# Both ends of attention in a two-layer hybrid kernel: loads of the first head, inputs and weights of the output projection, order of its rows

## The chip, the cores and the metric

The kernel runs on one core of one Trainium2 chip. The metric is the device time of one execution in microseconds (us). One core has five engines with an instruction queue each: TensorE (PE, with its weight loads shown apart as PEld), VectorE (DVE), ScalarE (ACT), GpSimd (POOL) and SyncE (SP, which here only issues DMAs). Each queue runs its instructions in the order in which they stand; a semaphore wait in front of one holds all that stand behind it on that engine.

## What is computed

Two layers work on 256 context tokens and 1024 latent tokens of width 1024, in f32. Cut to what matters here:

```python
def layer(x, ctx):
    h = x * (1 + scale) + shift                    # the same for ctx, with its own vector
    ru, rg, aq, ak, av, ag, nq, nk, nv, ng = split(h @ w_in)
    yr = rwkv_bidirectional(ru)                    # 6 heads x 64: 384 columns
    ya = grouped_query_attention(aq, ak, av)       # 6 query and 2 key heads x 64: 384 columns
    yn = neighbourhood_attention(nq, nk, nv, rpb)  # 4 heads x 64: 256 columns
    y = concat(yr * silu(rg), ya * silu(ag), yn * silu(ng)) @ w_out
    return layer_norm(alpha * x + gate * y)
```

The first layer also updates the context tokens; the second gives the latent tokens alone.

## The kernel before, in words

Each layer goes through four stages: the input projections (`layer_proj`), the RWKV branch in waves of chained small steps (`rwkv`), the attention heads (`attention`), and the output projection with the norm (`out_weights`, `out_proj`). The stages are written one after the other, but the order on each engine is decided when the kernel is built: a scheduler simulates the program and places each instruction where it becomes ready, so the last waves run beside the first attention heads, and the first products of the output projection run inside the last attention heads. Pools of tiles reuse each other's addresses with waits by tile, so a tile of a later stage waits for the last reader of what lay there.

**First head of attention.** Heads come in the order 0, 1, 2, 3 (neighbourhood), then the two groups of query heads, G before H in layer 0 and H before G in layer 1. A head's keys and queries lie in DRAM as 64 rows; `dup` (L851) loads them twice into the two halves of a staging tile `stg` (L857, two DMAs), from ACT's queue for the first two calls of a layer and from SP's after that. `load_k` (L860) casts the tile to the reduced format fp32r (ACT, L865) and takes the remainder (POOL, L866); `load_q` (L869) does the same (L873, L874, L875). `na_head` (L1081) calls `load_k`, then `load_q`, then loads values and the two bias tables.

**Between the two.** Each head's last steps (`inv`, `spread`, `gate`) turn sums of the softmax into factors (L1010, L1012, L1015, L1023), multiply (L1025) and store 64 rows of the result to `yg_d` (L1033). `yg_d` has eight rows of 128 features: rows 0 to 2 come from the RWKV branch (L806), 3 to 5 from the grouped heads, 6 and 7 from the neighbourhood heads.

**Output projection.** `out_weights` (L1131) loads `wout` as eight blocks of 128 output features (m0 to m7), 512 KB each, into a staging pool of four buffers (L1137), casts them on ACT (`wh`, L1140) and takes the remainder `wl` on DVE and POOL in turn (L1141). `out_proj` (L1144) goes over blocks of 256 tokens in the order 2, 3, 4, 1 and, in layer 0 alone, 0. For a block, `fetch` loads the eight rows k of `yg_d` one by one (`yf`, 128 KB, two buffers, L1157), casts them (`yh`, ACT, L1160) and takes the remainder (`yl`, POOL, L1161). Each product of an m and a k is three matmuls: yh by wh, yl by wh, yh by wl (L1186, L1187, L1188). The first half of a block is m0 to m3, the second m4 to m7; L1194 adds the half to the residual `s`, 1 MB, three buffers, loaded at L1281. The norm follows (`norm`, and `norm_last` with L1244 for the last block). What sets the order around the change:

```python
kord = (6, 3, 4, 5, 0, 1, 2, 7)                 # rows k of yg_d, in the order of fetch and of the sums
order = [2, 3, 4, 1] + ([] if last else [0])
```

**RWKV.** The wave step `wave_pre` (L555) has a tile `lp` (L578) in the pool `r2`; the blocks of the branch's output with odd number use the same place as `yb` (L772).

## Time and profile before

| | |
|---|---|
| time, median of 3 runs | 2469.1 us (2462.72 to 2471.28) |
| the profiled execution | 2478.63 us, of it 2476.9 us from the first to the last instruction |
| granted clock of TensorE, mean | 0.937 |
| TensorE matmul busy | 2189.6 us (88%) |
| VectorE busy | 1625.1 us (66%) |
| ScalarE busy | 1003.5 us (41%) |
| GpSimd busy | 1184.1 us (48%) |
| DMA | 298.17 MB, 120 GB/s in the mean |
| attention of layer 0 begins, layer 0's output projection follows it | at about 550 us, 1190 us |
| attention of layer 1 begins, layer 1's output projection follows it | at about 1783 us, 2341 us |

The page gives busy time by engine, a row of tenths by slice of the span, and the chain of work that ended last. Rows of the timeline read: start, duration, engine, line, operation, output and input, count; in brackets the engine's idle time before it and who ended it. A row with ACTq or SPq is the issue of DMAs from that queue. Windows give busy time by engine, the granted clock (PEclk, 1.00 is full) and the share of time in which the DMA engines were busy.

### The profile page before, as it was taken

The page shows a single profiled execution, that of the slowest core. Times are in us where ns is not written, and L with a number is a line of the kernel's source. Part 1 is how long each engine was busy: PE and PEld are TensorE (multiplying, and loading weights), DVE is VectorE, ACT ScalarE, POOL GpSimd, SP SyncE. Part 2 cuts the span into 40 slices and gives each one's busy share as a digit, 9 for nine tenths or more (in the row PEclk, how much of TensorE's full clock was granted, in tenths as well). Part 3 has the DMA queues.
Part 4 walks back from the last instruction along what each step waited for, and adds up shares of the span by engine and source line. Part 5 has one row for each costly group of instructions (what it writes and reads, how often), then busy time and mean ns, then how long its engine had stood idle before and what let it go on. Part 6 is the DMA issues. An engine that isn't in the chain of part 4 may idle for free.

```text
span 2476.9 us, 57781 instructions
## 1 busy us (share of the span) xinstructions
PE 2189.6 (88%) x22616; PEld 1645.0 (66%) x22616; DVE 1625.1 (66%) x3063; ACT 1003.5 (41%) x2186; POOL 1184.1 (48%) x1438
## 2 busy tenths in 40 slices
PE   6989999987888888989899999899868788989697
PEld 3777898765555555545897777787645555556397
DVE  5686423545768777775396785525468688778646
ACT  3333413334445454463233434223345444445522
POOL 4464426335555554462245456434456545545433
PEclk9999999996879999998999999999879999999899
DMA  7344335446555444351332445334555545332522
GB/s 281 112 162 164 111 92 123 120 108 139 126 116 136 114 100 119 102 177 34 101 103 91 146 161 182 107 90 121 141 116 140 102 99 117 84 90 64 161 71 94
DMA packets 448241, 298.17 MB, mean 120 GB/s; under 512 B 249600, under 2 KB 395880, under 8 KB 446944
## 3 DMA queue, kind: packets, MB, share of 16 engines
q1 hardware_dynamic: 439936, 281.71, 41.6%
q0 software_dynamic: 7392, 10.28, 1.5%
q8 instruction: 178, 2.92, 0.5%
q10 hardware_dynamic: 640, 2.49, 0.4%
q14 instruction: 95, 0.78, 0.1%
HBM read 198.37 MB, written 91.79 MB: 117 GB/s over the span
## 4 chain that ended last, share of the span: by engine, by line
PE 44%; DVE 21%; DMA 15%; issue 7%; ACT 6%; POOL 4%; SPq 3%; DVEq 0%; POOLq 0%; ACTq 0%
PE pj L203 5%; PE pj L204 5%; PE pj L205 5%; PE y L948 4%; DMA yf<-yg_d 3%; PE st L963 3%; PE sm L894 3%; DMA ls_d<-G 3%; DVE G L625 2%; PE st L964 2%; DVE mx L896 2%; DVE tmp L653 2%; PE ch L734 2%; PE py L754 1%; DMA lin<-ls_d 1%
## 5 line engine op out<-in xcount | busy, mean ns | idle before, releaser
L204 PE MATMUL pj<-hlo,wh 128*128 128x512 f32 (+1 forms) x1072 | 401.4, 375 | 14.3 <-DVE hlo L480 8.0
L203 PE MATMUL pj<-hhi,wh 128*128 128x512 f32 (+1 forms) x1072 | 403.2, 378 | 9.4 <-ACT qr L348 5.2
L205 PE MATMUL pj<-hhi,wl 128*128 128x512 f32 (+1 forms) x1072 | 400.6, 374 | 0.2 <-POOL wl L169 0.2
L204 PEld LDWEIGHTS pj<-hlo,wh 128*128 128x128 f32 x1072 | 205.0, 191 | 56.2 <-DVE hlo L480 8.3
L203 PEld LDWEIGHTS pj<-hhi,wh 128*128 128x128 f32 x1072 | 204.4, 191 | 54.8 <-issue 6.8
L169 POOL TENSOR_TENSOR wl<-wf,wh 128x512 fp32r<-128x512 f32 x104 | 143.8, 1387 | 202.2 <-ACT wh L168 178.7
L896 DVE TENSOR_REDUCE mx<-sm 128x1 f32<-128x512 f32 (+1 forms) x372 | 198.8, 554 | 50.1 <-PE sm L894 47.6
L205 PEld LDWEIGHTS pj<-hhi,wl 128*128 128x128 f32 x1072 | 204.9, 191 | 38.4 <-issue 3.3
L970 ACT ACTIVATE pt<-st 128x512 f32<-128x512 f32 (+1 forms) x292 | 164.9, 583 | 130.1 <-PE st L964 122.8
L948 PE MATMUL y<-pt,v 128*64 128x256 f32 (+1 forms) x1392 | 211.5, 398 | 2.3 <-ACT pt L973 1.4
L894 PE MATMUL sm<-k,q 128*128 128x256 f32 (+2 forms) x436 | 166.1, 422 | 25.8 <-DVE mx L896 19.5
L963 PE MATMUL st<-q,k 128*128 128x512 f32 (+3 forms) x376 | 165.0, 444 | 21.1 <-DVE rc L1012 5.9
L1186 PE MATMUL pj<-yh,wh 128*128 128x256 f32 x576 | 160.2, 290 | 24.4 <-ACT yh L1160 23.1
L1187 PE MATMUL pj<-yl,wh 128*128 128x256 f32 x576 | 164.0, 288 | 0.8 <-POOL yl L1161 0.8
L1188 PE MATMUL pj<-yh,wl 128*128 128x256 f32 x576 | 162.2, 286 | 0.0
L977 POOL TENSOR_TENSOR acc<-acc,pt 128x512 f32<-128x512 f32 x80 | 106.4, 1330 | 102.7 <-ACT pt L970 101.4
L948 PEld LDWEIGHTS y<-pt,v 128*64 128x64 f32 x1392 | 94.0, 142 | 89.6 <-issue 58.0
L964 PE MATMUL st<-q,k 65*128 65x512 f32 (+3 forms) x376 | 146.7, 393 | 1.9 <-ACT q L908 1.2
L894 PEld LDWEIGHTS sm<-k,q 128*128 128x128 f32 x436 | 80.6, 201 | 89.8 <-DVE mx L896 37.0
L625 DVE TENSOR_TENSOR G<-gt,msk 64x192 f32<-64x192 f32 (+1 forms) x320 | 110.5, 345 | 39.7 <-PE gt L620 28.4
L708 POOL MEMSET X<- 32x192 f32 x320 | 81.2, 254 | 102.0 <-PE py L754 74.6
L1186 PEld LDWEIGHTS pj<-yh,wh 128*128 128x128 f32 x576 | 109.9, 196 | 26.0 <-ACT yh L1160 23.5
(276 smaller groups left out, 5104.5 us busy)
## 6 DMA issues: line engine op xcount, KB each, us to landing
wf<-win SPq DMA_DIRECT2D x104, 256.0 KB
wm<-wmod SPq DMA_DIRECT2D x32, 512.0 KB
yf<-yg_d SPq DMA_DIRECT2D x72, 128.0 KB
wt<-wm SPq DMA_DIRECT2D x8, 1024.0 KB
gate_d<-o SPq DMA_DIRECT2D x32, 256.0 KB
wf<-wout SPq DMA_DIRECT2D x16, 512.0 KB
ldkk<-rw_d SPq DMA_DIRECT2D x40, 192.0 KB
ldkd<-rw_d SPq DMA_DIRECT2D x40, 192.0 KB
```

Of the source, the lines that this page charges most:

```text
L203: nc.tensor.matmul(out=ps[:, :n], lhsT=wh, rhs=hhi[:, k, t0:t0 + n], start=(k == 0), stop=False)
L204: nc.tensor.matmul(out=ps[:, :n], lhsT=wh, rhs=hlo[:, k, t0:t0 + n], start=False, stop=False)
L205: nc.tensor.matmul(out=ps[:, :n], lhsT=wl, rhs=hhi[:, k, t0:t0 + n], start=False, stop=(k == KT - 1))
L894: nc.tensor.matmul(out=sp_[:, :o], lhsT=q[0][:, qc:qc + 128], rhs=k[0][:, c0:c0 + o], start=True, stop=True)
L896: nc.vector.tensor_reduce(out=mx[:, n_:n_ + 1], in_=sp_[:, :o], op=ALU.max, axis=AX.X)
L948: mm = nc.tensor.matmul(out=y[64 * i:64 * i + 64, a0:a1], lhsT=v[:, t, :], rhs=pt[:, p0:p0 + a1 - a0], start=start, stop=stop and at == le ...
L963: nc.tensor.matmul(out=o, lhsT=k[0][:, 128 * t:128 * t + 128], rhs=q[0][:, qa:qb], start=True, stop=False)
L964: mm = nc.tensor.matmul(out=o, lhsT=k[1][0:65, 128 * t:128 * t + 128], rhs=q[1][0:65, qa:qb], start=False, stop=True)
L970: nc.scalar.activation(out=pt[:, :w], in_=sp_[:, :w], func=AF.Exp)
L1186: nc.tensor.matmul(out=p_, lhsT=wh[m][:, k], rhs=yh, start=(x_ == 0), stop=False)
L1187: nc.tensor.matmul(out=p_, lhsT=wh[m][:, k], rhs=yl, start=False, stop=False)
L1188: nc.tensor.matmul(out=p_, lhsT=wl[m][:, k], rhs=yh, start=False, stop=(x_ == KT - 1))
```

## The change

Five edits go together:

1. In each layer's first neighbourhood head, the loads of k and q are both issued before the cast of k; the staging tiles are handed to `load_k` and `load_q`.
2. The tile `lp`, and `yb` in its place, lie in pool `r3` instead of `r2`.
3. In the last layer, the pool of `yf`, `yh`, `yl` is opened ahead of the weights' staging pool, so that it has addresses of its own. The staging pool has two buffers there instead of four, and `yf` eight instead of two.
4. The order of the rows k: layer 0 ends with 4 and 5, layer 1 with 3 and 4, the rows that the last attention heads write.
5. Each block's load of the residual `s` is ordered behind the block's last `yf` load so far.

```diff
-                lp = r2.tile([128, 3, 4, 33], F32, tag="lp", name="lp")
+                lp = r3.tile([128, 3, 4, 33], F32, tag="lp", name="lp")
...
             for i in range(2):
-                eng.dma_start(out=sg_[64 * i:64 * i + 64, c0:], in_=src[:, c0:])
-            return sg_
-
-        def load_k(h):
-            sg_ = dup(k_d[h])
+                ld = eng.dma_start(out=sg_[64 * i:64 * i + 64, c0:], in_=src[:, c0:])
+            return sg_, ld
+
+        def load_k(h, sg_=None):
+            sg_ = sg_ or dup(k_d[h])[0]
...
-        def load_q(h):
-            sg_ = dup(q_d[h], lo)
+        def load_q(h, sg_=None):
+            sg_ = sg_ or dup(q_d[h], lo)[0]
...
-            k, q, v = load_k(2 + h), load_q(6 + h), load_v(vn_d, 64 * h)
+            sk = sq_ = None
+            if not nl[0]:
+                sk, sq_ = dup(k_d[2 + h])[0], dup(q_d[6 + h], lo)[0]
+            k, q, v = load_k(2 + h, sk), load_q(6 + h, sq_), load_v(vn_d, 64 * h)
...
-        w0 = est.enter_context(tc.tile_pool(name=f"of{l}", bufs=4, reuse_waits="tile"))
+        last = l == DEPTH - 1
+        w3 = es.enter_context(tc.tile_pool(name=f"oy{l}", bufs=2, reuse_waits="tile")) if last else None
+        w0 = est.enter_context(tc.tile_pool(name=f"of{l}", bufs=2 if last else 4, reuse_waits="tile"))
...
-                yf = w3.tile([128, n], F32, tag="yf", name="yf", bufs=2)
-                nc.sync.dma_start(out=yf, in_=yg_d[k, :, t0:t0 + n])
+                yf = w3.tile([128, n], F32, tag="yf", name="yf", bufs=8 if last else 2)
+                got[b] = nc.sync.dma_start(out=yf, in_=yg_d[k, :, t0:t0 + n])
...
-        kord = (6, 3, 4, 5, 0, 1, 2, 7)
+        kord = ((6, 7, 3, 0, 1, 2, 4, 5), (6, 7, 5, 0, 1, 2, 3, 4))[l]
...
-            nc.sync.dma_start(out=s, in_=x_src[:, :, 256 * b:256 * b + n])
+            follow(nc.sync.dma_start(out=s, in_=x_src[:, :, 256 * b:256 * b + n]), got[b])
```

No engine gets more or fewer instructions. The order changes within attention and output projection of both layers. In the changed kernel the lines of the output projection stand 7 to 10 lower: L1144 for L1137, L1166 for L1157, L1196 to L1198 for L1186 to L1188, L1291 for L1281. Three places follow.

On ACT, where attention of layer 0 begins, before (X, rsb and yst belong to the last RWKV waves; the bracket names the semaphores that the instruction waits on):

```order
L857 DMA stg<-k_d 64x1280 [waits DMAHW1_49]
L857 DMA stg<-k_d 64x1280 [waits DMAHW4_49]
L716 COPY rsb<-ch 128x192 [waits DVE_49,PE_49,Activation_49]
L865 CAST k_9985<-stg 128x1280 [waits DMAHW4_49,DMAHW6_49,DMAHW1_49,DMAHW0_49]
L857 DMA stg<-q_d 64x1280 [waits DMAHW5_49]
L730 COPY X_2966<-ch 32x3x64 [waits PE_49]
L730 COPY X_2966<-ch 32x3x64 x2
L857 DMA stg<-q_d 64x1280 [waits DMAHW7_49]
L873 CAST q_9991<-stg 128x1280 [waits DMAHW7_49,DMAHW5_49]
```

The same place of the changed kernel:

```order
L857 DMA stg<-k_d 64x1280 [waits DMAHW1_49]
L857 DMA stg<-k_d 64x1280 [waits DMAHW4_49]
L857 DMA stg<-q_d 64x1280 [waits DMAHW6_49,DMAHW0_49,DVE_49]
L716 COPY rsb<-ch 128x192 [waits DVE_49,PE_49,Activation_49]
L857 DMA stg<-q_d 64x1280 [waits DMAHW0_49]
L865 CAST k_9988<-stg 128x1280 [waits DMAHW4_49,DMAHW1_49]
L730 COPY X_2966<-ch 32x3x64 [waits PE_49]
L730 COPY X_2966<-ch 32x3x64 x2
L873 CAST q_9991<-stg 128x1280 [waits DMAHW6_49,DMAHW0_49]
L874 COPY q_9992<-q_9991 64x1280 [waits Activation_49]
```

Both loads of q moved up from behind the cast of k; the first now waits on a DVE semaphore and two DMA semaphores of its own.

On PE, right behind the last attention instruction of layer 0 (`tb`), before. The number behind pj names the block m (13764 is m3, 13877 is m4), that behind yh the row k in the order of fetch (13699 the first, 13705 the second, 13711 the third):

```order
L1023 MATMUL tb_13615<-c_ident_62,rb_13612 128x128 x4
L1186 MATMUL pj_13764<-yh_13699,wh_13654 128x256
L1187 MATMUL pj_13764<-yl_13700,wh_13654 128x256
L1188 MATMUL pj_13764<-yh_13699,wl_13655 128x256
L1186 MATMUL pj_13764<-yh_13705,wh_13654 128x256
L1187 MATMUL pj_13764<-yl_13706,wh_13654 128x256
L1188 MATMUL pj_13764<-yh_13705,wl_13655 128x256
L1186 MATMUL pj_13764<-yh_13711,wh_13654 128x256
L1187 MATMUL pj_13764<-yl_13712,wh_13654 128x256
L1188 MATMUL pj_13764<-yh_13711,wl_13655 128x256
L1186 MATMUL pj_13877<-yh_13699,wh_13660 128x256
```

And of the changed kernel, from twelve matmuls further on, with the fifth, sixth and seventh row (13723, 13729, 13735):

```order
L1196 MATMUL pj_13764<-yh_13723,wh_13654 128x256
L1197 MATMUL pj_13764<-yl_13724,wh_13654 128x256
L1198 MATMUL pj_13764<-yh_13723,wl_13655 128x256
L1196 MATMUL pj_13764<-yh_13729,wh_13654 128x256
L1197 MATMUL pj_13764<-yl_13730,wh_13654 128x256
L1198 MATMUL pj_13764<-yh_13729,wl_13655 128x256
L1196 MATMUL pj_13764<-yh_13735,wh_13654 128x256
L1197 MATMUL pj_13764<-yl_13736,wh_13654 128x256
L1198 MATMUL pj_13764<-yh_13735,wl_13655 128x256
L1196 MATMUL pj_13877<-yh_13699,wh_13660 128x256
```

Behind attention, m3 now takes seven rows before m4 begins, where it took three. Ahead of `tb`, among the instructions of the last heads, the products of m0 to m2 stand with the first three rows before (27 matmuls) and with the first seven in the changed kernel (63 matmuls); the one row left is the last in order.

On SP, at the end of attention of layer 1, before:

```order
L1137 DMA wf<-wout 128x1024 [waits DMAHW4_49]
L806 DMA yg_d<-yo 128x3x128 [waits DMAHW5_49,DVE_49,Activation_49]
L1137 DMA wf<-wout 128x1024 [waits DMAHW6_49,DMAHW1_49,DVE_49]
L1137 DMA wf<-wout 128x1024 [waits DMAHW7_49,DMAHW2_49,Pool_49]
L1137 DMA wf<-wout 128x1024 [waits DMAHW3_49,DMAHW0_49,DVE_49]
L1137 DMA wf<-wout 128x1024 [waits DMAHW4_49,Pool_49]
L1033 DMA yg_d<-gtl 64x512 [waits DVE_49]
L1033 DMA yg_d<-gtl 64x512
L1281 DMA s<-x_d 128x8x256 [waits DMAHW2_49,DMAHW3_49,PE_49,Pool_49]
L1281 DMA s<-x_d 128x8x256 [waits DMAHW5_49,PE_49,Activation_49]
L1281 DMA s<-x_d 128x8x256 [waits DMAHW6_49]
L1157 DMA yf<-yg_d 128x256 [waits DMAHW7_49]
```

And of the changed kernel:

```order
L1144 DMA wf<-wout 128x1024 [waits DMAHW4_49,DMAHW3_49,DMAHW5_49,PE_49,Pool_49]
L1166 DMA yf<-yg_d 128x256 x2
L1166 DMA yf<-yg_d 128x256 [waits DMAHW6_49]
L1166 DMA yf<-yg_d 128x256 [waits DMAHW7_49]
L1166 DMA yf<-yg_d 128x256 [waits DMAHW0_49]
L1166 DMA yf<-yg_d 128x256
L1166 DMA yf<-yg_d 128x256 [waits DMAHW2_49]
L1144 DMA wf<-wout 128x1024 [waits DMAHW3_49,DVE_49]
L1033 DMA yg_d<-gtl 64x512 [waits DMAHW4_49,DVE_49]
L1033 DMA yg_d<-gtl 64x512 [waits DMAHW5_49]
L1144 DMA wf<-wout 128x1024 [waits DMAHW6_49,Pool_49]
L1166 DMA yf<-yg_d 128x256 [waits DMAHW7_49,DMAHW4_49]
```

Seven loads of `yf` moved from behind the last attention store and three residual loads to ahead of that store; of the eight weight loads three instead of eight stand ahead of it, the other five behind.

More of the change, by code (lines that the diff above doesn't have):

```diff
@@ L771, in out_load @@
             if odd:
-                y, yb = r3.tile([128, 6, 64], F32, tag="ldkk", name="yo", bufs=1), r2.tile([128, 6, 64], F32, tag="lp", name="yo")
+                y, yb = r3.tile([128, 6, 64], F32, tag="ldkk", name="yo", bufs=1), r3.tile([128, 6, 64], F32, tag="lp", name="yo")
             else:
@@ L1141, in out_weights @@
             (nc.vector, nc.gpsimd)[m % 2].tensor_tensor(out=wl[m], in0=wf, in1=wh[m], op=ALU.subtract)
-        return w1, wh, wl
+        return w1, wh, wl, w3
     def out_proj(l, so, ow, x_src, x_dst, hd):
@@ L1146, in out_proj @@
         last = l == DEPTH - 1
-        w1, wh, wl = ow
-        w3 = so.enter_context(tc.tile_pool(name=f"oy{l}", bufs=2, reuse_waits="tile"))
+        w1, wh, wl, w3 = ow
+        if w3 is None:
+            w3 = so.enter_context(tc.tile_pool(name=f"oy{l}", bufs=2, reuse_waits="tile"))
         pj = [so.enter_context(tc.tile_pool(name=f"oj{l}", bufs=3, space=PSUM))]
@@ L1151, in out_proj @@
         NY = 10
+        got = {}
         def fetch(b, ys, ks):
```

## The prediction

> **What bounds the kernel now.** I read the chain of work that ended last first, for the shares.
>
> ```profile
> PE 44%; DVE 21%; DMA 15%; issue 7%; ACT 6%; POOL 4%; SPq 3%; DVEq 0%; POOLq 0%; ACTq 0%
> ```
>
> TensorE sets most of the span, but DMA's 15% are stretches in which PE stands still for a transfer. So I asked for windows around the two ends of attention (columns: window, its length, busy time of PE, PEld, DVE, ACT, POOL, granted clock, DMA share, GB/s).
>
> ```profile
> 550.00:600.00 50.00, 29.90 (x580) 22.48 (x574) 28.11 (x79) 16.31 (x37) 21.20 (x27) 0.59 0.68 146
> 600.00:650.00 50.00, 43.08 (x710) 28.94 (x709) 44.12 (x120) 22.51 (x59) 28.86 (x43) 0.93 0.51 112
> 1109.00:1200.00 91.00, 80.11 (x483) 50.55 (x482) 43.27 (x78) 32.56 (x64) 23.18 (x19) 0.89 0.25 77
> 551.00:557.00 6.00, 1.69 (x48) 1.41 (x48) 4.93 (x13) 0.00 (x0) 3.49 (x6) 0.80 1.03 264
> 561.00:571.00 10.00, 4.74 (x239) 4.06 (x228) 3.20 (x7) 1.12 (x4) 2.40 (x8) 0.67 0.96 176
> 1783.00:1798.00 15.00, 8.44 (x105) 6.67 (x97) 6.15 (x10) 3.52 (x11) 6.63 (x12) 0.54 1.08 248
> 2357.00:2360.40 3.40, 3.40 (x16) 3.40 (x17) 0.00 (x0) 0.63 (x2) 1.60 (x3) 0.51 0.27 77
> 2360.40:2370.00 9.60, 9.60 (x82) 9.60 (x81) 0.00 (x0) 2.03 (x5) 4.23 (x6) 1.00 0.27 78
> ```
>
> Where attention of layer 0 begins (550 to 600), PE is busy 29.9 us of 50, where the next 50 us have 43.1: 13.2 us are missing. The DMA engines are full at the same time (1.03, 0.96), and again where layer 1's attention begins (1.08). Then PE's waits at the two output projections, layer 0 first:
>
> ```profile
> PE pj L1186 <- ACT yh L1160: 5.9, 1, 5.9
> ...
> PE pj L1186 <- ACT yh L1160: 17.1, 1, 17.1
> ```
>
> One wait of 5.9 us and one of 17.1 us, both for the first projection inputs: 23 us of PE's time with nothing beside it.
>
> **The change, part by part.** The sums are made against the profiled execution, 2478.6 us (2476.9 of span, 1.7 around it), which lies 9.5 us above the median of 2469.1; I take the differences as the same and apply them to the median. About 0.3%, 7.4 us, is what a measurement can tell from no change.
>
> *A, start of layer 0's attention.* The timeline of ACT:
>
> ```profile
> 551.11 0.46 ACTq L857 DMA_DIRECT2D stg<-k_d  x1
> 557.42 1.26 ACT L865 CAST k<-stg 128x1280 fp32r<-128x1280 f32 x1
> 561.14 0.45 ACTq L857 DMA_DIRECT2D stg<-q_d  x1
> 570.52 1.26 ACT L873 CAST q<-stg 128x1280 fp32r<-128x1280 f32 x1 [8.86 <-DMA stg<-q_d]
> ```
>
> k was issued until 551.6 and was there at 557.4, after 5.8 us. q was issued at 560.2 and 561.1 only because its DMAs stood behind k's cast, and ACT waited 8.9 us for it. In the changed order q's DMAs are the next on ACT's queue, at about 552. Landing behind k it needs another 5.8 us (563.2) or, as measured, 9.4 us (566.8): q comes 3.7 to 7.3 us sooner. What is late next are the waves' own loads, which compete for the full engines; PE's waits from 545 to 620 show them:
>
> ```profile
> PE ch L713 <- DMA X<-vt_d: 7.0, 3, 5.0
> ...
> PE sm L894 <- POOL q L875: 1.8, 1, 1.8
> ```
>
> Bytes that q takes earlier are taken from X. Bounds: 0 (X comes later by as much) and -9 us (the whole wait). I take -4, near the lower landing estimate. The added DVE wait on q's first DMA is for the gate stores, whose addresses it reuses; behind it on ACT stand rsb and k's cast, and its price is inside the bounds.
>
> *B, start of layer 1's attention.*
>
> ```profile
> 1788.98 0.45 ACTq L857 DMA_DIRECT2D stg<-k_d  x1
> ...
> 1797.93 1.26 ACT L865 CAST k<-stg 128x1280 fp32r<-128x1280 f32 x1 [7.57 <-DMA stg<-k_d]
> 1797.93 1.10 ACTq L857 DMA_DIRECT2D stg<-q_d  x2
> ...
> 1804.71 1.04 ACT L873 CAST q<-stg 128x1024 fp32r<-128x1024 f32 x1 [1.51 <-DMA stg<-q_d]
> ```
>
> Here k itself came late, at 1797.9, its second half being issued behind a step that waited for the waves' data; q followed 6.8 us later. With the engines at 1.08 until 1798, q's bytes can only delay k or the waves; what is saved is at most the 6.8 us between k and q. Bounds: +2 (k later by what the q load puts in its way, a third of that) and -6; I take -2.
>
> *C, layer 0's output projection.* SP issued the residual ahead of the late rows, and ACT waited 10.2 us for them. PE's matmuls at full clock come 0.12 us apart, and two rows through the two `yf` buffers come 3.3 us apart (chain):
>
> ```profile
> 1190.68 3.07 SPq L1281 DMA_DIRECT2D s<-xT  x3
> ...
> 1203.01 0.74 ACT L1160 CAST yh<-yf 128x256 fp32r<-128x256 f32 x2 [10.15 <-DMA yf<-yg_d]
> ...
> 1191.02 0.28 PE L1187 MATMUL pj<-yl,wh 128*128 128x256 f32 x1
> 1191.14 0.28 PE L1188 MATMUL pj<-yh,wl 128*128 128x256 f32 x1
> ...
> 1204.25 2.03 DMA yf<-yg_d
> ...
> 1207.56 1.89 DMA yf<-yg_d
> ```
>
> In the changed order only the last row (k = 5) waits for attention; behind `tb` stand the products of m3 to m6 with rows that are there already, and the residual goes behind the row. So the wait of 5.9 us goes. Besides, 63 instead of 27 projection matmuls run within attention's tail: 36 x 0.12 = 4.3 us, which can go into the 10.9 us that PE idles from 1109 to 1200. Together 10.2 at best; at least 3, if the matmuls in the tail only push attention's and half of the wait stays. I take -7.
>
> *D, the last projection.* The chain and the timeline, from the last store to the end of block 2's second half (L1194 adds a half):
>
> ```profile
> 2334.85 3.37 DVE L1141 TENSOR_TENSOR wl<-wf,wh 128x1024 fp32r<-128x1024 f32 x1
> ...
> 2338.26 2.17 DVE L1141 TENSOR_TENSOR wl<-wf,wh 128x1024 fp32r<-128x1024 f32 x1
> ...
> 2341.55 2.50 DMA yg_d<-gtl
> ...
> 2347.17 9.24 DMA yf<-yg_d
> ...
> 2356.94 1.86 PE L1186 MATMUL pj<-yh,wh 128*128 128x256 f32 x7 [17.15 <-ACT yh L1160]
> ...
> 2380.68 1.66 DVE L1194 SCALAR_TENSOR_TENSOR s<-pj,gm,s 128x256 f32<-128x256 f32 x4 [8.90 <-PE pj L1188]
> ```
>
> Before, the inputs came behind 3 MB of residual and took 9.2 us. Now seven rows are loaded ahead of the last store, and fewer remainders stand on DVE ahead of `rc` and `gtl`: the two shown took 5.5 us beside POOL's, so attention ends perhaps 3 us sooner. PE can begin at about 2340. Block 2 is 192 matmuls x 0.12 = 23 us, so it could end at 2363.5 instead of 2380.7: -17 at best. But its weights now pass through two staging buffers. Their prices (min/median/max in ns, casts on ACT, remainders on DVE and POOL), and the last four loads before:
>
> ```profile
> L1140 ACT CAST wh<-wf x16: 1037/1045/1057, 1099.2 to 2343.1; 128x1024 fp32r<-128x1024 f32 x16
> ...
> L1141 POOL TENSOR_TENSOR wl<-wf,wh x8: 2349/2371/2794, 1102.3 to 2344.2; 128x1024 fp32r<-128x1024 f32 x8
> ...
> 2331.58 7.48 SPq L1137 DMA_DIRECT2D wf<-wout  x4
> ...
> 2343.06 1.04 ACT L1140 CAST wh<-wf 128x1024 fp32r<-128x1024 f32 x1 [0.21 <-DMA wf<-wout]
> ```
>
> The last of four was issued by 2339.1 and landed at 2343: a load takes some 4 us (estimate from these two rows). A turn of POOL's buffer is 4 + 1.05 + 2.37 = 7.4 us. With m1 done at 2338, m3, m5 and m7 come at 2345.4, 2352.8 and 2360.2, and about 4 us later where 1 MB residual loads share the engines: 2364. The products of m7 then end near 2367, while PE fills its waiting with block 3, which has its own rows early thanks to the eight buffers. So about 2368 instead of 2380.7: -12. Bounds -3 (below) and -17.
>
> PE's clock shows 0.51 in the first 3.4 us behind the 17 us wait, then 1.00. The Trainium skill, page "TensorE: Matmul & The Clock Gate", Part 1 on the HAM clock gate, puts PE at half clock after an idle window of about 3.4 us until it has been busy as long; by that rule the half-clock stretch would go with the wait, and D would be -14 rather than -12, an estimate that the sum leaves out.
>
> *At nothing.* `lp` in `r3` changes addresses and no instruction. The residual behind the inputs is needed only at the first add (2370 before, some 2353 now), 1 MB at the 264 GB/s of the first window is 4 us, and seven PSUM banks let PE go on if it is late; without that cover it would cost those 4 us. The remaining reordering of attention has no row of its own; PE's longest single stall from 1100 to 1190 is the first of these two waits, and I bound it by plus or minus 4 us a layer, taken as 0:
>
> ```profile
> PE sm L894 <- DVE mx L896: 3.7, 2, 3.5
> ...
> PE pj L1186 <- DVE gtl L1025: 0.8, 1, 0.8
> ```
>
> Sum: -4 - 2 - 7 - 12 = -25 us, from 2469.1 to 2444.
>
> **The rivals.** *First: the starts don't carry.* DMA shares of 1.03, 0.96 and 1.08 speak for it: what q gains X and the bias tables lose, and A and B are 0. -7 - 12 = -19, 2450 us. Against it: ACT had nothing else to do for 8.9 us, and PE's only wait for X there was 7.0 us. The Trainium skill, page "DMA: Bandwidth & Descriptors", section "Issuing engines are not separate DMA queues", says that transfers started from ACT, SP or GpSimd run on the same 16 engines and interleave; the full windows agree, and by the rule alone this rival would be the forecast.
>
> *Second: the two staging buffers become the bound.* Should a weight load take 9.2 us, as the `yf` load behind the residual did, a turn is 12.7 us, and m7 comes at 2338 + 3 x 12.7 = 2376; its products end at 2378: D is -3, the sum -16, 2453 us. For it: five loads now stand behind residuals and inputs. Against it: they are spread over 30 us in which DMA was at 0.27.
>
> *Third: the last layer's inputs don't come early.* The seven loads stand behind a weight load that waits for PE and POOL; if that is released only by attention's last matmuls, they are issued at about 2339, as the last weight load was, and land after 4 us or a little more. PE then begins some 5 us later than 2340: D is about -7, the sum -20, 2449 us. For it: the wait on PE is new; against it: `wf` needs no more than one attention tile's place.
>
> *Fourth, slower: projection matmuls hold attention in layer 0.* PE's queue is in order, and 63 projection matmuls on seven rows now stand among the last heads'. A row through two buffers is 3.3 us where POOL is free, and POOL's additions in attention are 1.33 us each:
>
> ```profile
> L977 POOL TENSOR_TENSOR acc<-acc,pt 128x512 f32<-128x512 f32 x80 | 106.4, 1330 | 102.7 <-ACT pt L970 101.4
> ```
>
> With one of them ahead of each remainder seven rows take 7 x 4.6 = 32 us; if PE stands for all of it, C is +32 instead of -7, and the sum +14: 2483 us. It decides from 25 us of such waits on (18 from the other terms, 7 of the bound). Against it: 27 such matmuls stood there before, and the only wait of theirs from 1100 to 1190 is the 0.8 us above.
>
> **How the numbers follow.** The forecast has 0.42, the first rival 0.22, the second 0.16, the third 0.10, the fourth 0.10. The predicted time is the forecast's, 2444 us. Adding bounds as if independent (A 4.5, B 4, C 3.5, D 7, reordering 8) gives 12.6; with the rivals at 2449 to 2453 above it, and the fourth left out, the range is 2427 to 2464. Faster than 2461.7 end nearly all of the forecast and some 85% of the first three rivals: 0.80. Within 0.3%: 0.11. Slower: the fourth, as far as it decides: 0.09.
>
> **What would show it.** A: q's cast at 563 to 567, PE's busy time from 550 to 600 at 33 us or more. B: q's cast 2 to 6 us behind k's. C: no wait of pj for yh above 1 us behind `tb`, no pj wait above 2 us in the tail. D: first pj behind `tb` within 2 us, block 2's last add 10 to 14 us sooner relative to `tb`, no PE wait for wl above 3 us. The forecast is wrong if the time is above 2464, or if the gain sits in other places than C and D.

## The result and the profile after

The changed kernel takes 2450.7 us (median of 7 runs, 2443.12 to 2462.52), the kernel before 2472.72 us (median of 7, 2462.72 to 2486.47). The ratio on record is 0.9898 with a 95% interval of 0.9878 to 0.9918, or 25 us less (20 to 30); the two medians alone differ by 22 us (0.9911), inside that interval. The span of the profiled execution went from 2476.9 to 2447.7 us, 29.2 us less. The predicted 2444 us started from the median of 3 runs, 2469.1, which is 3.6 us lower than the median of 7.

The page's chain of waits has this line now (shares of the span by engine; the chain could be followed back through less of the span than before, so only the order of the shares is compared):

```profile
PE 23%; DVE 12%; DMA 5%; ACT 3%; issue 3%; POOL 2%; SPq 1%; DVEq 0%; ACTq 0%; POOLq 0%
```

DMA stays third, with 5 beside PE's 23 where it had 15 beside 44. The windows of the changed kernel that answer to those in the prediction, and two at the last projection (columns as there):

```profile
550.00:600.00 50.00, 33.36 (x632) 25.18 (x636) 28.62 (x85) 19.24 (x46) 23.54 (x30) 0.63 0.72 165
...
1783.00:1798.00 15.00, 9.86 (x131) 7.50 (x130) 5.82 (x14) 6.62 (x16) 10.45 (x13) 0.61 0.98 236
...
551.00:557.00 6.00, 2.50 (x57) 2.07 (x48) 5.74 (x13) 0.96 (x4) 5.00 (x7) 0.93 1.02 267
...
561.00:571.00 10.00, 5.89 (x270) 5.00 (x268) 3.04 (x8) 3.77 (x6) 5.75 (x4) 0.67 0.83 202
...
2318.00:2330.00 12.00, 6.16 (x26) 5.23 (x27) 4.25 (x6) 6.58 (x14) 8.00 (x8) 0.62 0.85 278
...
2340.00:2357.00 17.00, 14.82 (x118) 14.21 (x118) 4.19 (x9) 5.75 (x11) 6.92 (x6) 1.00 0.40 135
```

PE is busy for 3.5 us more at the start of layer 0's attention, 33.4 of 50. The DMA engines are about as full there as before (0.72 against 0.68). Before, PE did nothing from 2340 to 2357, the 17 us behind its last attention instruction. In the changed kernel that instruction stands at 2321.5, and PE is busy for 14.2 us of the 17 from 2322 to 2339 and for 14.8 of the 17 from 2340 to 2357.

**Start of layer 0's attention.** ACT's timeline, and PE's waits from 545 to 620:

```profile
558.81 0.45 ACTq L857 DMA_DIRECT2D stg<-q_d  x1
559.36 1.26 ACT L865 CAST k<-stg 128x1280 fp32r<-128x1280 f32 x1 [0.26 <-issue]
...
566.33 1.26 ACT L873 CAST q<-stg 128x1280 fp32r<-128x1280 f32 x1 [3.08 <-DMA stg<-q_d]
```

```profile
PE ch L713 <- DMA X<-vt_d: 3.5, 1, 3.5
...
PE sm L894 <- POOL q L875: 0.6, 1, 0.6
```

q's cast now follows k's after 7.0 us instead of 13.1, and the waves' wait for X did not grow: 3.5 us instead of 7.0. The loads of q were not issued at 552, as the prediction had it, but at 556.2 and 558.8, since the first waits on semaphores of its own and the second stands behind `rsb`.

**Start of layer 1's attention**, ACT again: both halves of q are issued before the steps that wait for the waves, and q's cast follows k's after 2.2 us instead of 6.8.

```profile
1785.62 0.45 ACTq L857 DMA_DIRECT2D stg<-q_d  x1
...
1792.86 1.26 ACT L865 CAST k<-stg 128x1280 fp32r<-128x1280 f32 x1 [6.35 <-DMA stg<-k_d]
...
1795.10 1.06 ACT L873 CAST q<-stg 128x1024 fp32r<-128x1024 f32 x1
```

**Layer 0's projection.** On SP the residual (L1291) is one load between inputs instead of three ahead of them, and among PE's waits from 1195 to 1300 there is none for yh; the longest of a projection matmul is 0.8 us:

```profile
1201.01 0.81 SPq L1166 DMA_DIRECT2D yf<-yg_d  x2
1201.86 0.63 SPq L1291 DMA_DIRECT2D s<-xT  x1
1204.29 8.62 SPq L1166 DMA_DIRECT2D yf<-yg_d  x5
```

```profile
PE pj L1196 <- DVE gtl L1025: 0.8, 1, 0.8
```

**The last projection.** PE's waits from 2318 to the end, SP's issues, and the adds of block 2 (four of the first half, then m4 to m7 one by one):

```profile
PE pj L1196 <- ACT wh L1147: 2.1, 2, 1.6
PE pj L1197 <- POOL yl L1170: 2.0, 1, 2.0
...
PE pj L1196 <- ACT yh L1169: 0.7, 1, 0.7
```

```profile
2317.06 3.28 SPq L1166 DMA_DIRECT2D yf<-yg_d  x7
...
2339.97 4.25 SPq L1144 DMA_DIRECT2D wf<-wout  x2
```

```profile
2339.86 1.65 DVE L1204 SCALAR_TENSOR_TENSOR s<-pj,gm,s 128x256 f32<-128x256 f32 x4
2343.88 0.48 DVE L1204 SCALAR_TENSOR_TENSOR s<-pj,gm,s 128x256 f32<-128x256 f32 x1 [2.36 <-PE pj L1198]
...
2356.91 0.48 DVE L1204 SCALAR_TENSOR_TENSOR s<-pj,gm,s 128x256 f32<-128x256 f32 x1 [3.12 <-PE pj L1198]
```

The wait of 17.1 us for yh is 0.7 us. What is left is in pieces of 2 us, for weights and for a remainder on POOL.

To see which stage gave what, both programs are cut at four marks: the first k cast of each layer's attention, and the last `tb` (L1023) of each layer, behind which nothing of attention is left for PE. The `tb` rows, two of before and two of after:

```profile
1185.21 0.66 PE L1023 MATMUL tb<-c_ident,rb 128*128 128x128 f32 x4 [1.04 <-ACT rb L1015]
...
2339.14 0.66 PE L1023 MATMUL tb<-c_ident,rb 128*128 128x128 f32 x4 [2.62 <-ACT rb L1015]
```

```profile
1197.23 0.66 PE L1023 MATMUL tb<-c_ident,rb 128*128 128x128 f32 x4 [1.04 <-ACT rb L1015]
...
2321.52 1.12 PE L1023 MATMUL tb<-c_ident,rb 128*128 128x128 f32 x4 [2.89 <-ACT rb L1015]
```

| stage, us | before | after | difference |
|---|---|---|---|
| layer 0: first k cast to last tb | 627.8 | 637.9 | +10.1 |
| last tb to layer 1's first k cast (projection of layer 0, input projections of layer 1) | 612.7 | 595.6 | -17.1 |
| layer 1: first k cast to last tb | 541.2 | 528.7 | -12.5 |
| last tb to the end | 137.8 | 126.2 | -11.6 |

The end gave what it should. But layer 0's attention became longer by 10 us, and layer 1's shorter by 12.5 us, which no term of the prediction has. PE's windows over the two attention stages, before and then the changed kernel, layer 0 first, show what these stages are made of:

```profile
557.42:1185.21 627.79, 540.63 (x7507) 347.26 (x7504) 453.11 (x1102) 305.77 (x731) 314.52 (x392) 0.89 0.47 115
559.36:1197.23 637.87, 558.17 (x7539) 359.45 (x7536) 455.30 (x1102) 308.43 (x734) 314.15 (x396) 0.87 0.46 114
```

```profile
1797.93:2339.14 541.21, 461.73 (x6893) 295.44 (x6893) 432.53 (x1016) 272.40 (x641) 292.93 (x373) 0.93 0.44 103
1792.86:2321.52 528.66, 461.07 (x6893) 296.75 (x6893) 420.16 (x1014) 269.52 (x636) 287.83 (x371) 0.93 0.44 104
```

PE's idle time, the length less the busy time, fell in both: from 87.2 to 79.7 us in layer 0 and from 79.5 to 67.6 in layer 1. In layer 0 PE's busy time grew by 17.5 us all the same. The 36 more products are 4.3 us of that; the rest goes with the granted clock, 0.87 instead of 0.89 (540.6 x 0.89 / 0.87 is 553, an estimate). The experiments were made to see which edit does what.

### The profile page after: what moved, and what is told of

The parts are those of the page before. It is cut to its first block, busy times and chain, and to the rows that moved or that the text cites. A ratio compares the mean times of both kernels' runs of the same rounds, so it can differ in the third digit from the quotient of the medians.

```text
span 2447.7 us, 57800 instructions
## 1 busy us (share of the span) xinstructions
PE 2206.0 (90%) x22616; PEld 1657.5 (68%) x22616; DVE 1615.7 (66%) x3063; ACT 1005.5 (41%) x2186; POOL 1180.5 (48%) x1438
## 5 line engine op out<-in xcount | busy, mean ns | idle before, releaser
L204 PE MATMUL pj<-hlo,wh 128*128 128x512 f32 (+1 forms) x1072 | 402.8, 376 | 13.1 <-DVE hlo L480 7.6
L963 PE MATMUL st<-q,k 128*128 128x512 f32 (+3 forms) x376 | 165.9, 445 | 12.5 <-issue 3.5
L1196 PE MATMUL pj<-yh,wh 128*128 128x256 f32 x576 | 162.8, 291 | 4.0 <-ACT wh L1147 2.1
L1198 PE MATMUL pj<-yh,wl 128*128 128x256 f32 x576 | 163.2, 288 | 0.1
L977 DVE TENSOR_TENSOR acc<-acc,pt 128x512 f32<-128x512 f32 x112 | 101.7, 918 | 30.3 <-ACT pt L970 29.8
```

Source lines behind the costliest of these rows:

```text
L204: nc.tensor.matmul(out=ps[:, :n], lhsT=wh, rhs=hlo[:, k, t0:t0 + n], start=False, stop=False)
L963: nc.tensor.matmul(out=o, lhsT=k[0][:, 128 * t:128 * t + 128], rhs=q[0][:, qa:qb], start=True, stop=False)
L977: eng.tensor_tensor(out=acc[i][:, :w], in0=sums[i][:, :w], in1=pt[:, :w], op=ALU.add)
L1196: nc.tensor.matmul(out=p_, lhsT=wh[m][:, k], rhs=yh, start=(x_ == 0), stop=False)
L1198: nc.tensor.matmul(out=p_, lhsT=wl[m][:, k], rhs=yh, start=False, stop=(x_ == KT - 1))
```

## The experiments

All times are ratios to the kernel before, measured beside each kernel; us are worked out against its median there (2476 to 2477 us, in the changed kernel's row 2472.7). The changed kernel has its ratio from runs of its own, so a difference between it and a variant carries both intervals, 8 to 11 us together. Ratio and interval are those on record; the quotients of the medians lie up to 0.0024 beside them. The stages come from one profile each. How far two profiles of one order differ can be read from kernels whose order is the same up to the last head: layer 0's first k cast to last `tb` took 637.9, 641.8, 632.9 and 629.8 us in the changed kernel and its three variants of the last projection, so a stage alone carries some 6 us to either side.

| kernel | ratio (95%) | us | L0 k cast to tb | tb to L1 k cast | L1 k cast to end | of it behind tb |
|---|---|---|---|---|---|---|
| before | 1 | | 627.8 | 612.7 | 679.0 | 137.8 |
| changed | 0.9898 (0.9878 to 0.9918) | -25 | 637.9 | 595.6 | 654.8 | 126.2 |
| edit 1 alone | 0.9992 (0.9964 to 1.002) | -2 | 627.9 | 608.5 | 677.2 | 138.3 |
| edit 2 alone | 1.0048 (1.0024 to 1.0072) | +12 | 626.1 | 609.7 | 688.2 | 125.3 |
| edit 3 alone | 0.9963 (0.9939 to 0.9988) | -9 | 629.7 | 611.2 | 670.8 | 132.5 |
| edit 4 alone | 0.9959 (0.9928 to 0.9991) | -10 | 642.8 | 597.1 | 676.1 | 122.8 |
| edit 5 alone | 1.0037 (1.0004 to 1.007) | +9 | 633.0 | 603.1 | 698.6 | 125.3 |
| without edit 1 | 0.9961 (0.9936 to 0.9987) | -10 | 643.6 | 594.9 | 677.3 | 123.8 |
| without edit 2 | 0.9909 (0.9877 to 0.994) | -23 | 632.7 | 591.9 | 676.1 | 127.6 |
| edit 1 in layer 0 alone | 0.9959 (0.9933 to 0.9985) | -10 | 637.7 | 592.7 | 680.7 | 113.2 |
| old rows in layer 0 | 0.9972 (0.9944 to 0.9999) | -7 | 633.9 | 602.6 | 674.7 | 124.3 |
| old rows in layer 1 | 0.9912 (0.9883 to 0.9942) | -22 | 632.9 | 591.0 | 664.8 | 128.9 |
| no edit 5 in layer 1 | 0.9909 (0.9871 to 0.9946) | -23 | 629.8 | 589.2 | 668.8 | 132.5 |
| four staging buffers | 0.9906 (0.9875 to 0.9937) | -23 | 641.8 | 585.4 | 664.4 | 126.8 |

The five edits alone add up to -2 + 12 - 9 - 10 + 9 = 0 us; together they give -25. No sum over the edits explains the change.

The last column needs care. In the kernel before and in the changed kernel no product of layer 1's projection stands ahead of the last `tb`, but in the profiles of edit 2 alone 18 of its matmuls do, and of edit 1 in layer 0 alone 63, so that less work is left behind it. And edits 4 and 5 alone, with at most 3 such matmuls and without edit 3, leave 122.8 and 125.3 us behind `tb`, no more than the changed kernel's 126.2; but their attention of layer 1 ended 12 and 32 us later behind its first k cast than before's. A stage that ends sooner behind a later mark need not be a gain.

**Edit 1 alone.** The lines that set the order (cut; the rest hands the tiles on):

```diff
+            if not nl[0]:
+                sk, sq_ = dup(k_d[2 + h])[0], dup(q_d[6 + h], lo)[0]
```

> Edit 1 alone: k and q of the first head issued together in both layers, all else as before. Theory (the early q doesn't carry; what counts in attention is the order that comes out): q's cast in layer 0 comes about 4 us sooner, but the last tb of layer 0 comes no sooner than before or up to 8 us later; layer 1's attention, from the first k cast to the last tb (541 us before), is some 8 us shorter, since its order is nearly that of the changed kernel. Time 2460 to 2475. Rival (the starts carry, as predicted): the last tb of layer 0 about 4 us sooner, layer 1's 2 us more, time about 2466 with both gains still standing at the last tb.

Measured: ratio 0.9992 (the medians, 2469.2 us against 2477.1, give 0.9968, inside the interval). ACT's rows at the start, and the last tb of layer 0:

```profile
557.80 1.26 ACT L865 CAST k<-stg 128x1280 fp32r<-128x1280 f32 x1 [0.48 <-issue]
563.26 1.26 ACT L873 CAST q<-stg 128x1280 fp32r<-128x1280 f32 x1 [1.79 <-DMA stg<-q_d]
```

```profile
1185.65 0.66 PE L1023 MATMUL tb<-c_ident,rb 128*128 128x128 f32 x4 [1.04 <-ACT rb L1015]
```

q comes 7 us sooner, and attention ends at 1185.7 where it ended at 1185.2. The early q does not carry. Its window shows where it went:

```profile
557.80:1185.65 627.85, 548.71 (x7501) 353.75 (x7498) 452.21 (x1102) 307.04 (x730) 314.28 (x392) 0.88 0.46 115
```

PE is idle for 8.1 us less than before in that stage (79.1 against 87.2) and busy for 8.1 us more, with the same work at a granted clock of 0.88 instead of 0.89. The other half of the expectation failed: layer 1's attention took 539.0 us, not 8 less than 541.2.

**All but edit 1.** The lines above taken out of the changed kernel.

> All of the change but edit 1: the first head's q is issued behind k's cast again. Theory: the two projections give their gains (some 10 us behind tb in layer 0 against before, 11 to 12 us behind tb in layer 1), and attention comes out as its order happens to: time within 8 us of the changed kernel on either side, with q's cast at 570 again. Rival (the starts carry): 6 us slower than the changed kernel, with layer 0's last tb 4 us later than in the changed kernel.

Measured: 0.9961, some 15 us slower than the changed kernel (0.9898), more than either theory allowed. Layer 0's attention takes 643.6 us, and layer 1 up to the end 677.3 instead of 654.8. So edit 1, worth 2 us by itself, is worth 15 beside the others. (Both differences come with the other order that the edit brings, not with the early q alone.)

**Edit 3 alone.**

```diff
+        w3 = es.enter_context(tc.tile_pool(name=f"oy{l}", bufs=2, reuse_waits="tile")) if last else None
+        w0 = est.enter_context(tc.tile_pool(name=f"of{l}", bufs=2 if last else 4, reuse_waits="tile"))
...
+                yf = w3.tile([128, n], F32, tag="yf", name="yf", bufs=8 if last else 2)
```

> Edit 3 alone: inputs' pool ahead of the weights' staging pool, eight yf buffers and two staging buffers in the last layer; old row order, residual as before. Up to the last head the order is that of before. Theory (own addresses for the inputs are enough only together with the row order): two rows are loaded sooner, the third row, written last, still stands ahead of the others; PE's wait of 17 us behind the last tb shrinks to 8 to 14, time 3 to 8 us less than before. Rival A (the pools are the whole of the gain at the end): 11 to 12 us less. Rival B (two staging buffers cost more than the inputs gain): 0 to 5 us slower than before.

Measured: 0.9963, 9 us less (3 to 15); behind the last tb 132.5 instead of 137.8, 5.3 us. The theory had 3 to 8 us of time, so the profile's share fits and the measured time is just above. But it did not come by a wait for yh of 8 to 14 us: that wait is gone, and waits for weights stand in its place. The first of PE's waits from 2330 on:

```profile
PE pj L1189 <- ACT wh L1142: 6.3, 5, 2.4
```

**Four staging buffers** in the changed kernel.

```diff
-        w0 = est.enter_context(tc.tile_pool(name=f"of{l}", bufs=2 if last else 4, reuse_waits="tile"))
+        w0 = est.enter_context(tc.tile_pool(name=f"of{l}", bufs=4 if last else 4, reuse_waits="tile"))
```

> The changed kernel with four staging buffers for the last layer's weights instead of two; the order is the same up to the last head. Theory (the turns of the two buffers set when m4 to m7 come, whose adds stand at 2343.9, 2349.6, 2353.3 and 2356.9): m7's add comes 5 us sooner or more, time 2 to 5 us below the changed kernel. Rival (the DMA engines, at 0.98 from 2330 to 2340, set it): the weights only change places with the inputs, m7's add moves by less than 2 us, time within 2 us of the changed kernel.

Measured: 0.9906 against 0.9898, 126.8 us behind tb against 126.2. The adds of block 2's halves stand 19.4 and 30.9 us behind tb, the second row being four adds in 1.66 us, of which m7's is the last, at some 32.1. So m7 is about 3 us sooner than in the changed kernel (35.4), and still nothing is gained:

```profile
2344.20 1.66 DVE L1201 SCALAR_TENSOR_TENSOR s<-pj,gm,s 128x256 f32<-128x256 f32 x4 [6.61 <-PE pj L1195]
2355.71 1.66 DVE L1201 SCALAR_TENSOR_TENSOR s<-pj,gm,s 128x256 f32<-128x256 f32 x4 [9.85 <-PE pj L1195]
```

```profile
2330.00:2345.00 15.00, 12.80 (x92) 12.60 (x93) 4.08 (x7) 5.36 (x8) 14.99 (x13) 0.82 0.82 280
```

The two staging buffers do delay m4 to m7, but PE fills that time with block 3 (14.8 us busy of 17 above). With four, POOL is full (14.99 of 15 us), with remainders of weights and inputs in one stretch. Both theories put the decision in the wrong place, and m7's 3 us lie between their numbers; the rival's number for the time was nearer (2 us, from ratios that differ by less than their intervals).

**Edit 1 in layer 0 alone**, the other edits as in the changed kernel.

```diff
-            if not nl[0]:
+            if not nl[0] and not last:
```

> The changed kernel with edit 1 in layer 0 alone: same order as the changed kernel up to layer 1's attention, whose first q is again issued behind k's cast. Theory (the early q matters in layer 1 only through the order that comes out of it): layer 1's attention, first k cast to last tb, takes 545 to 555 us, as without edit 1 at all (553.5), where the changed kernel took 528.7 and 537.6; time 8 to 20 us above the changed kernel. Rival (the early q itself gives the 5 us by which it comes sooner): q's cast 5 us later against k's, and 2 to 6 us above the changed kernel.

Measured: 0.9959, 15 us above the changed kernel, as the theory had it. Layer 1 took 680.7 us from its first k cast to the end, against 654.8; but its attention took 567.5 us, where the theory had 545 to 555, with all 63 early products of the projection inside it and 113.2 us left behind it. q's cast follows k's after 8.7 us instead of 2.2. A delay of 6.5 us at the start of a stage does not by itself make it 26 us longer; the order behind it is another (that it is the order is argued here, and shown by the next kernel).

**Old row order in layer 0's projection.**

```diff
-        kord = ((6, 7, 3, 0, 1, 2, 4, 5), (6, 7, 5, 0, 1, 2, 3, 4))[l]
+        kord = ((6, 3, 4, 5, 0, 1, 2, 7), (6, 7, 5, 0, 1, 2, 3, 4))[l]
```

> The changed kernel with the old row order (6, 3, 4, 5, 0, 1, 2, 7) in layer 0's projection: 27 instead of 63 products stand in attention's tail. Theory (products in the tail push attention back by 10 to 14 us, and are given back behind tb): first k cast to the last tb of layer 0 takes 628 to 632 us instead of 638 to 642, and from there to layer 1's first k cast 605 to 611 instead of 585 to 596; both together within 6 us of the changed kernel. Rival (as predicted, the wait of 5.9 us and 4.3 us of products are saved): both together 7 to 10 us longer, with the wait for yh of some 6 us back behind tb.

Measured: layer 0's attention 633.9, then 602.6, both outside the theory's ranges. Together they are 1236.5, 3 us more than the changed kernel's profile (1233.5), which fits the theory, but 10 us more than the mean of the six kernels with its order there (1226.4, below), which fits the rival's 7 to 10. The wait for yh is 0.4 us although the rows are the old ones, so the rival's wait did not come back: it was the residual's place (edit 5) that removed it. The kernel is nevertheless 18 us slower than the changed one (0.9972 against 0.9898), and 20 us of that lie in layer 1 (674.7 against 654.8; 11.5 against the mean of the four kernels with the changed kernel's order, 663.2), which this edit doesn't touch.

**Old row order in layer 1's projection.** The same line with the second tuple old.

> The changed kernel with the old row order (6, 3, 4, 5, 0, 1, 2, 7) in layer 1's projection alone; up to the last head the order is that of the changed kernel. The row that is written last stands third. Theory (the row order is half of the gain at the end, as edit 3 alone gave 5.3 us of 11.6): from the last tb to the end 130 to 133 us instead of 126, time 4 to 7 us above the changed kernel. Rival (the weights, not the rows, set the end): 126 to 128 us and no difference.

Measured: 128.9 us behind tb against 126.2, time 0.9912, within the interval of the changed kernel. That is between the two expectations. The rows are worth some 3 us at the end in these two profiles, no more than profiles differ.

**No edit 5 in layer 1.**

```diff
-            follow(nc.sync.dma_start(out=s, in_=x_src[:, :, 256 * b:256 * b + n]), got[b])
+            ld = nc.sync.dma_start(out=s, in_=x_src[:, :, 256 * b:256 * b + n])
+            if not last:
+                follow(ld, got[b])
```

> The changed kernel without edit 5 in layer 1: the residual's loads may go ahead of the inputs in the last projection; the order is the same up to the last head. Theory (own addresses and eight buffers let the inputs go first anyway): tb to the end 125 to 129 us, time within 3 us of the changed kernel. Rival (residual ahead of the inputs was the wait of 17 us): tb to the end 131 us or more, a PE wait for yh of over 5 us.

Measured: 132.5 us behind tb, time 0.9909. The longest wait is for weights, not inputs (PE's waits from 2312 on), because two residuals go ahead of the last weight loads on SP:

```profile
PE pj L1193 <- ACT wh L1145: 5.4, 1, 5.4
```

```profile
2326.18 1.27 SPq L1288 DMA_DIRECT2D s<-x_d  x2
2327.54 2.13 SPq L1142 DMA_DIRECT2D wf<-wout  x1
```

The inputs were early anyway, as the theory said, and the time is within its 3 us; its number for the end was too low by 4 us, for a wait that neither named. The rival's 131 us or more came true without its wait for yh.

**Edit 2 alone.** The line of `lp`; that of `yb` changes in the same way:

```diff
-                lp = r2.tile([128, 3, 4, 33], F32, tag="lp", name="lp")
+                lp = r3.tile([128, 3, 4, 33], F32, tag="lp", name="lp")
```

> Edit 2 alone: the tile lp in the other pool, an address and nothing else; the order up to layer 0's last head is that of before, layer 1's attention comes out in another order. Theory (layer 1's attention takes what its order happens to give): from its first k cast to the end, 679 us before, between 668 and 695, so up to 12 us off before on either side without any work added. Rival (an edit at nothing costs nothing, as predicted): within 4 us of before, in that stretch and in time.

Measured: 1.0048, 12 us slower (6 to 18), from moving an address. Layer 1 takes 688.2 us from its first k cast, as the theory allowed. PE's waits from there on, this kernel first, then before:

```profile
PE py L754 <- DVE tt L689: 14.1, 6, 3.9
...
PE mg L684 <- DVE di L687: 7.4, 2, 6.7
```

```profile
PE py L754 <- DVE tt L689: 7.2, 4, 4.0
...
PE mg L684 <- DVE di L687: 3.2, 2, 2.5
```

The RWKV waves wait 11 us longer for DVE's small steps. But other waits are shorter, and the windows from the first k cast to the last `tb` (this kernel, then edit 5 alone) show that waiting is not what makes this stage longer:

```profile
1795.23:2358.08 562.85, 487.56 (x6923) 312.37 (x6919) 428.35 (x1021) 277.56 (x645) 300.28 (x377) 0.88 0.42 102
1795.21:2368.49 573.28, 495.48 (x6933) 315.28 (x6932) 435.97 (x1023) 276.06 (x643) 292.64 (x379) 0.88 0.42 101
```

PE is idle for 75.3 us here and 77.8 with edit 5 alone, less than before's 79.5. It is busy for 26 and 34 us longer, at a granted clock of 0.88 instead of 0.93: 461.7 x 0.93 / 0.88 is 488 us (an estimate), and 487.6 and 495.5 were measured. The runs show it as well as the profile: the granted clock over the whole execution has a median of 0.924 in the ten runs of edit 2 alone and 0.926 in those of edit 5 alone, and 0.934 in the kernel before, measured beside them. So the new order costs time mainly by running nearly the same PE work at a lower clock.

**Edit 4 alone**, both row orders new.

> Edit 4 alone: the new row orders of both projections. Theory (edit 5, not the rows, takes the wait for yh away; the rows move products into attention's tail): behind layer 0's last tb a wait for yh of 3 to 6 us stays; first k cast to last tb 632 to 640 us, from there to layer 1's first k cast 598 to 606, both together 3 to 8 us below before's 1240.5; at the end no more than 4 us gained; the time also follows layer 1's order, 2460 to 2480. Rival (the rows carry the gain in layer 0): no wait for yh above 1 us, both together 10 to 15 us shorter, time about 2462.

Measured: 0.9959. The wait for yh is 0.5 us, so the rows too remove it: either edit does so by itself, and the theory's 3 to 6 us was wrong. Layer 0's attention is 15.0 us longer and the stretch behind it 15.6 us shorter: 1239.9 together, against 1240.5, where theory and rival had 3 to 8 and 10 to 15 us less. At the end 122.8 us are left behind tb, 15 less than before, where the theory had 4 at most. Of the 15.0 us in layer 0, 11.6 are busy time of PE (552.2 us against 540.6; 4.3 for the products, the rest with a granted clock of 0.88 instead of 0.89) and 3.4 idle time. The wait in question (PE's waits from 1185 on):

```profile
PE pj L1186 <- ACT yh L1160: 0.5, 1, 0.5
```

**Edit 5 alone.**

> Edit 5 alone: each residual load behind the block's last input load so far. Theory (the residual ahead of the last rows was layer 0's wait): the wait for yh of 5.9 us falls below 1 us, from layer 0's last tb to layer 1's first k cast 603 to 608 us instead of 612.7; the time follows layer 1's order as well, 2460 to 2478. Rival (only the new row order takes the wait away): 4 us or more of it stay, 610 to 613 us.

Measured: no wait for yh is left, and the stretch behind tb is 603.1 us, both as the theory had it. SP loads five inputs ahead of the first residual:

```profile
1195.88 7.18 SPq L1158 DMA_DIRECT2D yf<-yg_d  x5
1203.12 0.63 SPq L1282 DMA_DIRECT2D s<-xT  x1
```

Yet the kernel is 9 us slower than before (1.0037), outside what was expected: layer 1 takes 698.6 us, the longest of all, at the low clock shown above.

**All but edit 2.** `lp` and `yb` stay in `r2`.

> All of the change but edit 2; in layer 1's attention most instructions stand as in the changed kernel. Theory (an address does nothing by itself, and the order is nearly that of the changed kernel): first k cast of layer 1 to the end 655 to 669 us, as in the four kernels with that order, time within 6 us of the changed kernel. Rival (lp's place is what lets layer 1's waves and attention run together): that stretch 674 us or more, time 8 us or more above the changed kernel.

Measured: 0.9909, 3 us from the changed kernel and within its interval, so `lp`'s place is not what gives the gain. The stage failed the theory, 676.1 us, and fits the rival's 674 or more; the time does not. The profiled execution, 2464.4 us, is itself 9 us above the median of 2455.6.

## Why the prediction came out right, step by step

**The sum and the time.** -25 us were forecast and 25 measured (22 by the medians). The sum is partly right for the reasons given and partly by luck. Between the two profiles, 29.2 us apart, the stages of A and C gave -7.0 us where -11 was forecast, the end -11.6 where D had -12, and layer 1's attention -12.5 where only B's -2 was forecast; the first k cast came 1.9 us later. So 4 us that did not come and 10 that no term has stand against each other. The prediction's own last sign, that the gain sit in C and D, was met in part only: 12.5 of the 29.2 us lie elsewhere.

**D, -12 us:** 11.6 behind the last tb. The inputs came early and 17.1 us of waiting for them shrank to 0.7, as forecast. The weights were late much as worked out: m7's add stands 35.4 us behind tb, where the estimate (2368 with tb some 3 us sooner) had about 32. One sign of D failed: block 2's last add came some 7 us sooner relative to tb (from about 42.7 to 35.4), not 10 to 14; the rest of the 11.6 us lies with block 3, whose products fill the waits, the part of the working that mattered. Four buffers showed that the two-buffer turns delay m7 by some 3 us and cost nothing on balance, where the second rival had made them the bound. That edit 3 is what gave D is not shown: by itself it gave 5.3 us, edits 4 and 5 each shortened the wait of 17.1 us without it (to 2.0 and 5.5), and no kernel with all but edit 3 was run. The third rival didn't occur, since the seven loads were issued at 2317.1, ahead of the last tb.

**C, -7, and A, -4:** together -11, measured from the first k cast to layer 1's: -7.0 between the two profiles, and -14 in the mean of the six kernels that share this order or nearly so in layer 0 (1233.5, 1227.2, 1223.9, 1219.0, 1230.4, 1224.6: 1226.4, against 1240.5 before and 1240.9 in edit 3 alone). The split is another. A alone is nothing at the last tb, as the first rival had it: the step "I take -4" failed, and edit 1 alone showed it, with q 7 us sooner and tb at the same place. Both signs named for A came true (q's cast at 566.3, PE busy for 33.4 us), so they were no proof of a gain. Nor did the first rival's mechanism show: PE waited 5.1 us for X there, against 7.0 before, and was idle for 8 us less in the whole stage, but the lower clock took these back. C's wait of 5.9 us went, by the rows or by the residual's place, either being enough. The fourth rival's place was right and its mechanism not: layer 0's attention was 15 us longer with the new rows alone, without a long wait of a projection matmul, and the stretch behind gave 15.6 us back. Only together with edit 1 was the balance clearly positive. The 36 more products are 4.3 us at 0.12 us each, and the rest of the longer stage is mostly PE at a lower granted clock; why the clock was lower is open.

**B, -2:** q's cast came as forecast, 2.2 us behind k's, but edit 1 alone kept 1.8 us of it up to the end, which is less than two profiles differ.

**The reordering, "plus or minus 4 us a layer, taken as 0":** this step failed. In layer 1 the stretch from the first k cast to the end took 655 to 669 us in the four kernels with the changed kernel's order, 671 to 681 in eight others, before among them (679.0), and 688 and 699 with an address or the residual's place changed alone. The term is worth some 20 us to either side, not 4, and it decided the sign for edits 2 and 5. What it runs through was not in the prediction: less idle time of PE in the changed kernel (67.6 us against 79.5), and a lower granted clock in the slow orders. In the changed kernel it came out well: layer 1's attention is 12.5 us shorter between the two profiles, 5 us in the mean of the four (528.7, 537.6, 535.8, 536.2 against 541.2 and, in edit 3 alone with before's order, 538.3). **"`lp` at nothing"** failed with it: no work was added, and the order that follows from the address cost 12 us.

**Two rules of the Trainium skill.** In edit 1 alone the DMA share was 1.01 from 551 to 557 and 1.14 from 557 to 563; q came 7 us sooner, and the last tb did not. The Trainium skill, page "DMA: Bandwidth & Descriptors" (section "Issuing engines are not separate DMA queues"), says that DMAs started from ACT, SP or GpSimd run on the same 16 engines and interleave; the full windows agree.

The half-clock stretch did not go with the long wait. The granted clock was 0.99 from 2320 to 2320.9 and 0.50 from there to 2322, inside the wait of 2.9 us ahead of the last `tb`, which took 1.12 us instead of 0.66; waits of 0.7 and 2.0 us followed, and matmuls came 0.21 us apart until 2331. By the Trainium skill, page "TensorE: Matmul & The Clock Gate" (Part 1), which has half clock after an idle window of about 3.4 us, the prediction expected the stretch to go, for 2 us more; here less than that in one piece was enough. The rows:

```profile
2326.57 0.41 PE L1198 MATMUL pj<-yh,wl 128*128 128x256 f32 x1
2326.79 0.41 PE L1197 MATMUL pj<-yl,wh 128*128 128x256 f32 x1
...
2332.04 0.28 PE L1196 MATMUL pj<-yh,wh 128*128 128x256 f32 x1
2332.16 0.28 PE L1197 MATMUL pj<-yl,wh 128*128 128x256 f32 x1
```

**What stays open.** That layer 1 follows the order is shown best by the old rows in layer 0, which change nothing else there: its attention took 550.4 us against 529 to 538 in the four kernels with the changed kernel's order. In edits 2 and 5 alone the time goes with the granted clock; which placements lower the clock is not shown, nor which shorten PE's idle time in the changed kernel. An order fixed by hand, which would separate each edit from the scheduler, wasn't tried, and neither was the change without edit 3. None of the variants is measurably faster than the changed kernel.

## What to carry to other kernels

Where a scheduler sets the order, an edit's effect is its own plus that of a new order for everything behind it; here the second was up to 20 us, more than any edit's own. Split each stage of PE into idle time, busy time and granted clock before calling a wait the cause: edit 2 added 11 us of waits on DVE, and PE's idle time in that stage fell all the same. Cut both profiles at marks that every version has, and look for the gain in the stage where the edit works; a gain or a loss elsewhere belongs to the order. And ask of a wait that is to go how many things would remove it: the residual's place and the row order each did, so their gains don't add. A time counted from a mark says little where an edit moves the mark or moves work across it.

## What the runs showed of the hardware that wasn't expected

PE's clock fell to half within a single wait of 2.9 us (0.99 until 2320.9, 0.50 from there), in a stretch where PE was busy for only 2.4 of 8 us (2318 to 2326). It stayed there for 4.9 us of nearly unbroken matmuls (2326.2 to 2331.1); behind the wait of 17 us before, it was 3.4 us. Removing a long wait and leaving short ones did not bring the clock back.

Edits 2 and 5 alone, which add no work, moved the granted clock over a stage of some 550 us from 0.93 to 0.88, without more idle time of PE, and the stage's busy time followed it: 461.7 us at 0.93, 487.6 and 495.5 at 0.88.
